# Second feed-forward of an encoder step: block products from its first pair on, and the order of the sums in front of it

## The chip, the cores and the metric

The kernel runs on one core of a Trainium2 chip. The time is device microseconds of one execution. The kernel before took 1299.93 us (median of three executions, 1299.71 to 1300.36). The profile shown below is of one further execution, which took 1300.08 us; all durations that the prediction uses come from that one.

A core has five engines that run side by side and wait for each other through semaphores: TensorE (PE in the profile) multiplies, VectorE (DVE) and ScalarE (ACT) work element by element, GpSimd (POOL) and SyncE (SP) issue transfers here. Each engine does its own instructions strictly in the order in which the program lists them.

## The reference

One layer works on 576 columns (512 frames of a new stream, 64 of a running one) of 1024 features, in float32:

```
x = x + 0.5 * swiglu(rms_norm(x, ffn1_norm))          # first feed-forward
p = rms_norm(x, mix_norm) @ w_in                       # mixer: two gated convolutions
...
merged = sigmoid(gate_a) * y_a + sigmoid(gate_b) * y_b
x = x + merged @ w_out                                 # output projection of the mixer
x = x + 0.5 * swiglu(rms_norm(x, ffn2_norm))           # second feed-forward
y = rms_norm(x, final_norm)

rms_norm(x, g) = x * rsqrt(mean(x*x) + 1e-6) * g
swiglu(h)      = (silu(h @ w_gate) * (h @ w_up)) @ w_down      # 2816 hidden features
```

The change touches the last rows of the mixer (the projection by `w_out`) and the start of the second feed-forward.

## The kernel before

**Tiling.** Features lie on the 128 partitions, so x is eight tiles `X[0..7]` of 128x576, and the 2816 hidden features are 22 tiles, in groups of 5, 5, 6 and 6. A float32 value v is split into a high part `hi` (rounded to the matmul's type) and a low part `v - hi`, and a product is three matmuls: hi·hi, hi·lo, lo·hi, where the first factor is the weight. A plain product of a weight column with all eight inputs is 8 x 3 matmuls for each half of 288 columns: 48. Its result takes one PSUM tile of two banks; there are four such tiles.

**Pairs.** For one hidden tile the gate and the up product form a 2x2 block problem: two weight columns, two halves of the input features (tiles 0 to 3 and 4 to 7), two halves of the columns. `pair` computes it with seven block products instead of eight, each of 4 x 3 = 12 matmuls into one bank: 84 in place of 96. For this DVE adds weights (sums `s1` to `s4` of the four raw weight blocks a11, a12, a21, a22), and adds inputs (the "forms" `t1` to `t4`); PE multiplies in the order a11, s2, s1, s3, a12, s4, a22 with the right sides first half of tiles 0 to 3, t2, t1, t3, first half of tiles 4 to 7, second half of tiles 4 to 7, t4; then `steps` adds the seven results on DVE and ACT (`q1`, `u2`, `u4`, `u3`, and `gate`, which multiplies by 1/rms `R` and runs Silu on ACT). The rest of a pair (`up`, `hidden`, `parts`) is left in the list `rest`, one step of which follows each block of the next pair.

**Forms.** `Forms.scale` (ACT) multiplies an input tile by its gain; `combine(p)` (four DVE instructions of 128x288, then two casts on ACT) forms the two tiles that hold t1, t2 and t3, t4 for the inputs p and p+4; `split(p)` (two DVE subtractions) makes their low parts.

**Weights.** `Stream` prepares weights in units: SP loads raw tiles of 128x512 into six buffers (`RAWS`), ACT casts the high part, and the low part is made in one of two ways. With "dma", ACT writes -hi and POOL issues a transfer that adds the raw weight to it in SBUF; with "dve", DVE subtracts. Raw tiles use the first, sums of tiles the second. `Stream.lead(n)` is called each time PE takes unit n, and issues the work of six units ahead (`AHEAD_UNITS`): this is what puts weight instructions between the others on ACT and DVE, in the order in which the program calls them.

**Around the change.** The loop over `IN_TURN` = 0, 4, 1, 5, 2, 6, 3, 7 (line 1125) is the projection by `w_out`: for each j, 48 matmuls, then DVE adds the result to `X[j]`, ACT makes the high and DVE the low part of the scaled input `xg[j]`, ACT squares `X[j]` and DVE adds the squares up; behind every second j stand scalings, forms and splits. Then `ss.gather` adds the last square and splits the sum for PE, and the second feed-forward begins with a plain product for hidden tile 0 (gate in the order of `IN_TURN`, the sum over partitions and `rstd`, up), then pairs from tile 1 on (`PLAIN["f2"]` is 1).

The calls of the engines go through a wrapper, so the profile names line 83 (85 in the changed kernel) for nearly everything; tiles tell the instructions apart: `mm` is PSUM, `x` the residual, `act` inputs and their parts, `u` and `g` (and `act`) prepared weights, `raw` loaded weights, `w` sums of weights and scaled inputs, `tmp` and `acc` intermediate values, `r` 1/rms.

Of the kernel before, what the change touches and what calls it, by code (L numbers as in the profile page):

```python
# [13 lines left out]
P = 128  # L14
D = 1024
KT = D // P
# [4 lines left out]
KU = KT // 2  # L21
T = SEQ + DSEQ
H = T // 2
# [25 lines left out]
WARM = 10  # L49


PLAIN = {"f1": 4, "f2": 1}

IN_TURN = (0, 4, 1, 5, 2, 6, 3, 7)

# [51 lines left out]
def tile_encoder_step(  # L107
# [83 lines left out]
    def par(j, r, n=1):  # L191
        return gains[:, r : r + n, j] if r < R_CA else prm[:, r - R_CA : r - R_CA + n, j]
# [129 lines left out]
    def gu_col(part, i):  # L322
        return i * P + (DFF if part == "u" else 0)

    def plan_pair(f, gu, i):

        a21, a22, a11, a12 = (
            ws.raw(gu, h * KU * P, KU, gu_col(part, i)) for part in "ug" for h in range(2)  # L330
        )
        s1, s2, s3, s4 = (f"{f}{i}s{n}" for n in range(1, 5))
        plan[f, "s", i] = [
            ws.unit(src, KU, home("g"), low, sums)
            for src, low, sums in (
                (a11, "dma", ((s1, (a21, a22)),)),
                (s2, "dve", ((s2, (s1, a11)),)),
                (s1, "dve", ()),
                (s3, "dve", ((s3, (a11, a21)),)),
                (a12, "dma", ()),  # L340
                (s4, "dve", ((s4, (s2, a12)),)),
                (a22, "dma", ()),
            )
        ]

    def plan_ffn(f, gu, dn):
# [23 lines left out]
    def plan_mixer(name, w, col):  # L370
        plan_tile(name, w, 0, (KU, KU), col, "act")
# [32 lines left out]
    def chunks(name):  # L404

        got = []
        for n in plan[name]:
            w = ws.get(n)
            got += [(w, kk) for kk in range(ws.units[n][1])]
        return got  # L410


    work = []
# [14 lines left out]
    early = {}  # L428
# [129 lines left out]
    class Forms:  # L558
# [171 lines left out]
    def ffn(f, xg, sums, finish, forms, R=None, todo=()):  # L730
# [3 lines left out]


        def plain(i, hs):
            nonlocal R
            t, up = ttile(), (f, "u", i)
            ps = product((f, "g", i), xg, order=IN_TURN if f == "f2" and i == 0 else None)
            got = None if up in early else chunks(up)  # L740
            if R is None:
                R = rstd(sums)
            ups = product(up, xg, got=got)
            hs.append(None)
            at = len(hs) - 1

            def gate():
                dve.tensor_tensor(halves(t), ps, halves(R), op=ALU.mult)
                sca.activation(t, t, AF.Silu)

            def hidden():
                dve.tensor_tensor(halves(t), ups, halves(t), op=ALU.mult)
                hs[at] = high(t)

            def parts():
                hs[at] = hs[at], low(t, hs[at])

            if f == "f2":
                rest.extend((gate, hidden, parts))
                return  # L760
            gate()
            forming()
            hidden()
            forming()
            parts()
            forming()
# [4 lines left out]
                    step(p)  # L771

        def pair(i, hs, last):
            qu, uu, t, cu = (ttile() for _ in range(4))
            q1, u2, u3, u4 = half(qu, 0), half(qu, 1), half(uu, 0), half(uu, 1)
            q = []
# [10 lines left out]
            steps = (  # L787
                lambda: sca.copy(q1, q[0]),
                lambda: dve.tensor_tensor(u2, q[1], q1, op=ALU.subtract),
                lambda: dve.tensor_tensor(u4, q[2], u2, op=ALU.subtract),  # L790
                q7,
                lambda: dve.tensor_tensor(half(t, 0), q[4], q1, op=ALU.add),
                gate,
            )
            for n, xs in enumerate(bs):
                w = ws.get(plan[f, "s", i][n])
                q.append(bank()[:, :H])
                for k in range(KU):
                    (whi, wlo), (xh, xl) = w, xs[k]
                    for m, (l, r) in enumerate(((whi, xh), (whi, xl), (wlo, xh))):  # L800
                        pe.matmul(
                            q[n], l[:, k, :], r, start=k == m == 0, stop=k == KU - 1 and m == 2
                        )
                if n > 0:
                    steps[n - 1]()
# [450 lines left out]
```

## Time and profile before

| | |
|---|---|
| median of three executions | 1299.93 us |
| profiled execution | 1300.08 us, span 1298.3 us |
| PE busy | 1286.2 us (99%), 9754 matmuls |
| DVE busy | 892.1 us (69%) |
| ACT busy | 768.7 us (59%) |
| POOL busy | 380.7 us (29%) |

The chain that ended last is 94% PE. The shares are means over the whole program; the change lies between 857 us (the projection by `w_out` begins) and about 960 us (the first group of the second feed-forward is multiplied out). The rows of the timeline that the prediction quotes give start, duration, engine, line, operation, output and inputs with their shapes, the number of instructions merged into the row, and in brackets how long the engine was idle before it and for what.

### The profile page before, as it was taken

How to read it: one execution, taken by the hardware profiler on the slowest of the kernel's cores; microseconds unless marked ns; L12 is line 12 of the kernel's file. 1: busy time of each engine (PE TensorE's matmuls, PEld its weight loads, DVE VectorE, ACT ScalarE, POOL GpSimd, SP SyncE). 2: the span in 40 equal slices, each digit the busy share in tenths (PEclk: the TensorE clock that was granted, in tenths of full speed). 3: DMA queues.
4: the chain of work that ended last, by engine and by line, in shares of the span. 5: the costliest groups of instructions: out<-in, count | busy, mean ns of one | idle time of the engine just before them, and what ended most of it. 6: DMA issues, size and time to landing. Idle time of an engine off the chain costs nothing.

```text
span 1298.3 us, 25689 instructions
## 1 busy us (share of the span) xinstructions
PE 1286.2 (99%) x9754; PEld 1283.6 (99%) x9754; DVE 892.1 (69%) x1469; ACT 768.7 (59%) x1362; POOL 380.7 (29%) x481
## 2 busy tenths in 40 slices
PE   9999999999999999999999999999999999999997
PEld 9999999999999999999999999999999999999996
DVE  6848758748945999888885160336967848847955
ACT  7746646645677654555444674467665655654664
POOL 0042332232233454333321322222142242241231
PEclk9999999999999999999999999999999999999999
DMA  7397786896698898778875978776688697796784
GB/s 219 79 196 159 157 185 155 164 196 143 151 199 180 168 212 175 169 166 177 168 168 128 197 158 174 164 157 142 139 174 175 144 194 160 155 211 133 161 176 108
DMA packets 287516, 215.39 MB, mean 166 GB/s; under 512 B 15520, under 2 KB 250016, under 8 KB 287392
## 3 DMA queue, kind: packets, MB, share of 16 engines
q0 software_dynamic: 59184, 97.28, 45.7%
q1 hardware_dynamic: 226336, 115.49, 31.4%
q8 instruction: 77, 1.26, 0.4%
q10 hardware_dynamic: 1872, 0.97, 0.3%
q14 instruction: 47, 0.39, 0.1%
HBM read 113.81 MB, written 2.62 MB: 90 GB/s over the span
## 4 chain that ended last, share of the span: by engine, by line
PE 94%; issue 2%; DVE 2%; DMA 1%; ACT 1%; POOL 0%; DVEq 0%; POOLq 0%; ACTq 0%
PE mm L83 94%; DVE tmp L83 1%; DMA u<-raw 0%; DVE g L83 0%; ACT tmp L83 0%; DMA act<-raw 0%; DMA raw<-in_ffn_w_gate_up_dram 0%; DVE x L83 0%; ACT act L83 0%; DVE acc L83 0%; ACT r L83 0%; DVE act L83 0%; ACT w L83 0%; ACT L83 0%; DVEq L1246 0%
## 5 line engine op out<-in xcount | busy, mean ns | idle before, releaser
L83 PE MATMUL mm<-act,u 128*128 128x288 f32 x4686 | 661.1, 294 | 1.2 <-DMA u<-raw 1.2
L83 PEld LDWEIGHTS mm<-act,u 128*128 128x128 f32 x4686 | 631.1, 188 | 1.7 <-DMA u<-raw 1.7
L83 PE MATMUL mm<-act,g 128*128 128x288 f32 x2778 | 399.7, 294 | 0.5 <-DMA g<-raw 0.4
L83 PEld LDWEIGHTS mm<-act,g 128*128 128x128 f32 x2778 | 378.1, 188 | 0.9 <-DMA g<-raw 0.6
L83 PE MATMUL mm<-act,act 128*128 128x288 f32 (+2 forms) x2244 | 306.7, 293 | 0.2 <-DMA act<-raw 0.2
L83 PEld LDWEIGHTS mm<-act,act 128*128 128x128 f32 x2244 | 297.6, 188 | 0.4 <-DMA act<-raw 0.4
L83 POOL DMA_DIRECT2D u<-raw x199 | 173.9, 874 | 373.0 <-ACT u L83 306.3
L83 ACT CAST u<-raw 128x512 fp32r<-128x512 f32 (+2 forms) x203 | 116.2, 572 | 165.2 <-PE mm L83 122.3
L83 POOL DMA_DIRECT2D g<-raw x122 | 106.7, 875 | 310.2 <-ACT g L83 241.4
L83 DVE SCALAR_TENSOR_TENSOR w<-g,prm,w 128x606 f32<-128x606 f32 x232 | 179.3, 843 | 1.4 <-ACT w L83 1.4
L83 DVE TENSOR_TENSOR tmp<-mm,tmp 128x288 f32<-128x288 f32 (+1 forms) x239 | 107.7, 459 | 70.2 <-PE mm L83 52.1
L83 POOL DMA_DIRECT2D act<-raw x90 | 78.0, 866 | 199.1 <-ACT act L83 195.4
L83 ACT ACTIVATE u<-u 128x512 fp32r<-128x512 f32 (+2 forms) x199 | 117.9, 593 | 6.3
L83 ACT CAST g<-raw 128x512 fp32r<-128x512 f32 (+2 forms) x126 | 68.9, 547 | 39.2 <-DMA raw<-in_ffn_w_down_dram 14.5
L83 ACT CAST u<-w 128x512 fp32r<-128x512 f32 x79 | 48.9, 619 | 60.1 <-DVE w L83 51.4
L83 DVE SCALAR_TENSOR_TENSOR tmp<-mm,r 128x576 f32<-128x576 f32 x48 | 36.3, 756 | 68.2 <-PE mm L83 68.2
L83 ACT CAST g<-w 128x512 fp32r<-128x512 f32 x77 | 47.7, 619 | 57.6 <-DVE w L83 50.1
L83 ACT CAST act<-tmp 128x576 fp32r<-128x576 f32 x84 | 56.7, 675 | 40.8 <-DVE tmp L83 39.0
L83 DVE TENSOR_TENSOR act<-tmp,act 128x576 fp32r<-128x576 f32 x84 | 62.1, 754 | 18.8 <-ACT act L83 17.2
L83 ACT ACTIVATE g<-g 128x512 fp32r<-128x512 f32 (+2 forms) x122 | 69.2, 567 | 3.9
L83 DVE TENSOR_TENSOR w<-raw,raw 128x512 f32<-128x512 f32 x78 | 53.5, 686 | 15.9 <-DMA raw<-in_ffn_w_gate_up_dram 15.9
L83 ACT CAST act<-raw 128x512 fp32r<-128x512 f32 (+3 forms) x94 | 55.6, 592 | 10.3 <-PE mm L83 7.5
(88 smaller groups left out, 804.8 us busy)
## 6 DMA issues: line engine op xcount, KB each, us to landing
raw<-in_ffn_w_gate_up_dram SPq DMA_DIRECT2D x171, 256.0 KB, 3.4
u<-raw POOLq DMA_DIRECT2D x140, 256.0 KB, 4.1
raw<-in_w_in_dram SPq DMA_DIRECT2D x112, 256.0 KB, 3.6
act<-raw POOLq DMA_DIRECT2D x80, 256.0 KB, 4.2
raw<-in_ffn_w_down_dram SPq DMA_DIRECT2D x96, 192.0 KB, 3.6
g<-raw POOLq DMA_DIRECT2D x63, 256.0 KB, 3.9
u<-raw POOLq DMA_DIRECT2D x43, 192.0 KB, 4.4
g<-raw POOLq DMA_DIRECT2D x43, 192.0 KB, 4.5
```

Of the source, the lines that this page charges most:

```text
L83: return self.tc.keep_in_program_order(fn(*args, **kwargs))
```

## The change

- `PLAIN["f2"]` goes from 1 to 0: hidden tile 0 of the second feed-forward is a pair too.
- For that one pair the blocks are taken in the order `FORMS_LAST` = 0, 4, 5, 1, 2, 3, 6, that is a11, a12, s4 (which multiply the inputs themselves), then s2, s1, s3, a22 (which multiply forms). Its weights are prepared in that order. The sum of squares goes through PE behind the sixth block, and the pair's `gate`, which needs it, moves to the head of `rest`, behind the first block of the next pair.
- In the projection loop the scaled input for the forms is made right behind each `xg[j]`, ahead of the square; `split` follows `combine` sooner; behind the loop the last `combine` and `split` come ahead of the adding of the last square (`gather`).
- The weights of `w_out` are prepared in `u` and `g` tiles in place of `u` and `act` tiles.

The core of the diff:

```diff
-PLAIN = {"f1": 4, "f2": 1}
+PLAIN = {"f1": 4, "f2": 0}
+FORMS_LAST = (0, 4, 5, 1, 2, 3, 6)
...
+    def order_of(f, i):
+        return FORMS_LAST if (f, i) == ("f2", 0) else range(7)
...
+        sums = [(s1, (a21, a22)), (s2, (s1, a11)), (s3, (a11, a21)), (s4, (s2, a12))]
+        if order == FORMS_LAST:
+            before = {0: sums[:1], 4: sums[1:2], 5: sums[3:], 3: sums[2:3]}
...
-        plan_mixer(("o", j), w_out, j * P)
+        plan_tile(("o", j), w_out, 0, (KU, KU), j * P, "g")
...
-        def scale(self, p):
-            self.b[p] = [wtile(n=T) for _ in range(2)]
-            for b, j in zip(self.b[p], (p, p + KU)):
+        def scale(self, p, js=None):
+            for j in js or (p, p + KU):
+                b = wtile(n=T)
                 sca.activation(b, X[j], AF.Copy, scale=par(j, self.r_g))
+                self.b.setdefault(p, []).append(b)
...
+            order = order_of(f, i)
+            late = ()
+            if order == FORMS_LAST:
+                steps[5], late = (lambda: None), (gate,)
+            q = [None] * 7
+            for m, n in enumerate(order):
+                q[n] = block(ws.get(plan[f, "s", i][m]), bs[n])
+                if R is None and m == 5:
+                    R = rstd(sums)
+                if m > 0:
+                    steps[order[m - 1]]()
                 if rest:
                     rest.pop(0)()
...
-            rest.extend((up, hidden, parts))
+            rest.extend((*late, up, hidden, parts))
...
+        p = n // 2
+        forms.scale(p, (j,))
         ss.square(X[j])
-        ss.add(dve)
-        p = n // 2
-        if n % 2:
-            forms.scale(p)
-        elif p > 0:
+        if n < KT - 1:
+            ss.add(dve)
+        if n % 2 == 0 and p > 0:
             forms.combine(p - 1)
-            if p > 1:
-                forms.split(p - 2)
+        if n in (3, 5, 6):
+            forms.split((n - 2) // 2)
+
+    forms.combine(KU - 1)
+    forms.split(KU - 1)
+    ss.add(dve)
     ss.gather()
-    forms.combine(KU - 1)
-    forms.split(KU - 2)
-    forms.split(KU - 1)
```

**First place: DVE, while PE makes the last product of the projection (j = 7).** Before, from the adding of the squares of `X[3]` to the low part of `xg[7]`; the `tmp` rows of 128x288 are `combine(2)`, the two `act` rows behind them a `split`, `w` a sum of weights:

```order
L83 TENSOR_TENSOR acc_1708_10688<-acc_1708_10688,tmp_1795_11221 128x576
L83 TENSOR_TENSOR tmp_1796_11224<-w_1783_11147 128x288
L83 TENSOR_TENSOR tmp_1796_11224<-w_1784_11148,tmp_1796_11224 128x288
L83 TENSOR_TENSOR tmp_1797_11225<-w_1783_11147,w_1784_11148 128x288
L83 TENSOR_TENSOR tmp_1797_11225<-w_1784_11148,tmp_1796_11224 128x288
L83 TENSOR_TENSOR act_1800_11234<-tmp_1767_11062,act_1769_11068 128x576
L83 TENSOR_TENSOR act_1801_11236<-tmp_1768_11063,act_1770_11070 128x576
L83 TENSOR_TENSOR w_1803_11239<-w_1789_11183,raw_1776_11082 128x512
L83 TENSOR_TENSOR x7_95<-mm_1802_11238,x7_95 128x576
L83 SCALAR_TENSOR_TENSOR act_1809_11299<-x7_95,gains_84,act_1808_11298 128x576
```

Now, over the same stretch (`u_1792` is the low part of s2, `w_1804` the sum s3, `g_1807` the low part of s1):

```order
L85 TENSOR_TENSOR acc_1708_10688<-acc_1708_10688,tmp_1796_11220 128x576
L85 TENSOR_TENSOR tmp_1797_11223<-w_1769_11065 128x288
L85 TENSOR_TENSOR tmp_1797_11223<-w_1784_11148,tmp_1797_11223 128x288
L85 TENSOR_TENSOR tmp_1798_11224<-w_1769_11065,w_1784_11148 128x288
L85 TENSOR_TENSOR tmp_1798_11224<-w_1784_11148,tmp_1797_11223 128x288
L85 TENSOR_TENSOR act_1801_11233<-tmp_1797_11223,act_1799_11229 128x576
L85 TENSOR_TENSOR act_1802_11235<-tmp_1798_11224,act_1800_11231 128x576
L85 TENSOR_TENSOR u_1792_11187<-w_1776_11081,u_1791_11186 128x512
L85 TENSOR_TENSOR w_1804_11239<-raw_1749_10924,raw_1734_10841 128x512
L85 TENSOR_TENSOR g_1807_11244<-w_1763_11027,g_1806_11243 128x512
L85 TENSOR_TENSOR x7_95<-mm_1803_11237,x7_95 128x576
L85 SCALAR_TENSOR_TENSOR act_1811_11300<-x7_95,gains_84,act_1810_11299 128x576
```

Between the squares and `x7` two weight subtractions have been added, and the two low parts now belong to the same `combine` (they read `tmp_1797` and `tmp_1798`, and wait for ACT's casts of those).

**Second place: ACT, behind the scaled input 7.** Before, from the high part of `xg[7]` on (`tmp_1813` is the high part of the sum of squares, `g_1804` the cast of a raw weight):

```order
L83 CAST g_1804_11241<-raw_1776_11082 128x512
L83 ACTIVATE g_1805_11242<-g_1804_11241 128x512
L83 CAST u_1806_11270<-w_1803_11239 128x512
L83 ACTIVATE act_1808_11298<-x7_95,gains_84 128x576
L83 ACTIVATE tmp_1810_11302<-x7_95 128x576
L83 ACTIVATE w_1811_11304<-x3_91,gains_84 128x576
L83 ACTIVATE w_1812_11305<-x7_95,gains_84 128x576
L83 CAST tmp_1813_11308<-acc_1708_10688 128x576
```

Now (`g_1827`, `g_1828` are the high part and -hi of a22 of the first pair):

```order
L85 ACTIVATE act_1810_11299<-x7_95,gains_84 128x576
L85 ACTIVATE w_1812_11303<-x7_95,gains_84 128x576
L85 ACTIVATE tmp_1813_11305<-x7_95 128x576
L85 CAST act_1816_11313<-tmp_1814_11307 128x576
L85 CAST act_1817_11315<-tmp_1815_11308 128x576
L85 CAST tmp_1820_11321<-acc_1708_10688 128x576
L85 CAST g_1827_11333<-raw_1737_10872 128x512
L85 ACTIVATE g_1828_11334<-g_1827_11333 128x512
```

The casts of the last forms and of the sum of squares now stand ahead of the weight a22.

**Third place: ACT, at the first Silu of the second feed-forward.** Now (`tmp_1824` is the gate of the first pair, `raw_1840` is a11 of the third pair):

```order
L85 ACTIVATE r_1851_11454<-tmp_1849_11452 128x576
L85 CAST g_1853_11466<-w_1846_11433 128x512
L85 CAST u_1861_11491<-raw_1766_11034 128x512
L85 ACTIVATE u_1862_11492<-u_1861_11491 128x512
L85 ACT_TABLE_LOAD
L85 ACTIVATE tmp_1824_11328<-tmp_1824_11328 128x576
L85 CAST g_1867_11519<-raw_1840_11397 128x512
L85 ACTIVATE g_1868_11520<-g_1867_11519 128x512
```

Before, the row behind the table load was the Silu of the plain tile, and a cast of a raw weight stood behind that in the same way:

```order
L83 ACTIVATE r_1838_11406<-tmp_1836_11404 128x576
L83 CAST g_1846_11473<-raw_1763_11028 128x512
L83 ACTIVATE g_1847_11474<-g_1846_11473 128x512
L83 ACT_TABLE_LOAD
L83 ACTIVATE tmp_1823_11331<-tmp_1823_11331 128x576
L83 CAST u_1853_11501<-raw_1826_11336 128x512
L83 ACTIVATE u_1854_11502<-u_1853_11501 128x512
```

What moved here is the Silu's place in the work: its inputs are now complete only behind the last block of the first pair, and the program lists it behind the first block of the second.

More of the change, by code (lines that the diff above doesn't have):

```diff
@@ L325, in plan_pair, with plan_block @@
     def plan_pair(f, gu, i):
-        a21, a22, a11, a12 = (
+        plan_block((f, "s", i), [
             ws.raw(gu, h * KU * P, KU, gu_col(part, i)) for part in "ug" for h in range(2)
-        )
[L332 to L343, printed above, removed]
+        ], [home("g") for _ in range(7)], order=order_of(f, i))
+    def order_of(f, i):
+        return FORMS_LAST if (f, i) == ("f2", 0) else range(7)
+    def plan_block(name, raws, homes, order=range(7)):
+        a21, a22, a11, a12 = raws
+        s1, s2, s3, s4 = ((name, n) for n in range(1, 5))
+        units = (
+            (a11, "dma"), (s2, "dve"), (s1, "dve"), (s3, "dve"), (a12, "dma"), (s4, "dve"),
+            (a22, "dma"),
+        )
+        sums = [(s1, (a21, a22)), (s2, (s1, a11)), (s3, (a11, a21)), (s4, (s2, a12))]
+        if order == FORMS_LAST:
+            before = {0: sums[:1], 4: sums[1:2], 5: sums[3:], 3: sums[2:3]}
+        else:
+            before = {0: sums[:1], 1: sums[1:2], 3: sums[2:3], 5: sums[3:]}
+        plan[name] = [
+            ws.unit(units[n][0], KU, home, units[n][1], before.get(n, ()))
+            for n, home in zip(order, homes)
         ]
@@ L410, in chunks, with block @@
         return got
+    def block(w, xs):
+        q = bank()[:, :H]
+        for k in range(KU):
+            (whi, wlo), (xh, xl) = w, xs[k]
+            for m, (l, r) in enumerate(((whi, xh), (whi, xl), (wlo, xh))):
+                pe.matmul(q, l[:, k, :], r, start=k == m == 0, stop=k == KU - 1 and m == 2)
+        return q
     work = []
@@ L736, in plain @@
         def plain(i, hs):
-            nonlocal R
             t, up = ttile(), (f, "u", i)
[L739 to L743, printed above, removed]
+            ps = product((f, "g", i), xg)
+            ups = product(up, xg)
             hs.append(None)
@@ L756, in parts @@
                 hs[at] = hs[at], low(t, hs[at])
-            if f == "f2":
-                rest.extend((gate, hidden, parts))
-                return
             gate()
@@ L785, in gate @@
                 sca.activation(t, t, AF.Silu)
-            steps = (
+            steps = [
                 lambda: sca.copy(q1, q[0]),
@@ L793, in pair @@
                 gate,
[L794 to L805, printed above, removed]
+            ]
+            order = order_of(f, i)
[9 more added lines that the diff above has]
+                    steps[order[m - 1]]()
                 if rest:
```

2 lines of the change are left out of this document (1 added, 1 removed).

## The prediction

> **What bounds the kernel now.** First the page: what is busy, and the chain of waits.
>
> ```profile
> PE 1286.2 (99%) x9754; PEld 1283.6 (99%) x9754; DVE 892.1 (69%) x1469; ACT 768.7 (59%) x1362; POOL 380.7 (29%) x481
> PE 94%; issue 2%; DVE 2%; DMA 1%; ACT 1%; POOL 0%; DVEq 0%; POOLq 0%; ACTq 0%
> ```
>
> PE sets the end, so every matmul taken away is a gain, and every moment in which PE waits is a loss. Second, PE's own waits, and two stretches of 20 us, of which the first holds these waits (columns: PE, PEld, DVE, ACT and POOL busy with counts, granted clock, DMA share, GB/s).
>
> ```profile
> PE mm L83 <- DMA u<-raw: 1.2, 2, 0.8
> PE mm L83 <- DMA g<-raw: 0.4, 1, 0.4
> 60.00:80.00 20.00, 18.41 (x134) 17.71 (x133) 9.78 (x18) 13.54 (x31) 9.51 (x12) 1.00 0.84 166
> 920.00:940.00 20.00, 20.00 (x152) 19.92 (x151) 18.39 (x34) 13.62 (x25) 4.30 (x5) 1.00 0.72 163
> ```
>
> These 1.6 us, 18.41 busy of 20, lie where the first feed-forward goes over to pairs. At the same place in the second feed-forward PE does not wait at all; its timeline:
>
> ```profile
> 900.72 0.94 PE L83 MATMUL mm<-act,g 128*128 128x288 f32 x6
> ...
> 906.97 0.69 PE L83 MATMUL mm<-tmp,ones_r 128*128 128x288 f32 x4
> 907.50 3.32 PE L83 MATMUL mm<-act,g 128*128 128x288 f32 x24
> ...
> 913.82 1.74 PE L83 MATMUL mm<-act,g 128*128 128x288 f32 x12
> 915.39 1.76 PE L83 MATMUL mm<-act,u 128*128 128x288 f32 x12
> 917.00 1.74 PE L83 MATMUL mm<-act,g 128*128 128x288 f32 x12
> ```
>
> At 900.72 the projection has ended; the plain gate takes 6.25 us, the plain up product 6.32 us, and a block of 12 takes 1.57 or 1.61 us, 1.59 in the mean. Third, what feeds PE here, DVE:
>
> ```profile
> 894.68 0.76 DVE L83 TENSOR_TENSOR x<-mm,x 128x576 f32<-128x576 f32 x1 [1.92 <-PE mm L83]
> 896.29 0.82 DVE L83 SCALAR_TENSOR_TENSOR act<-x,gains,act 128x576 fp32r<-128x576 f32 x1 [0.85 <-ACT act L83]
> 897.02 0.75 DVE L83 TENSOR_TENSOR acc<-acc,tmp 128x576 f32<-128x576 f32 x1
> 897.69 0.45 DVE L83 TENSOR_TENSOR tmp<-w 128x288 f32<-128x288 f32 x1
> ...
> 899.29 1.42 DVE L83 TENSOR_TENSOR act<-tmp,act 128x576 fp32r<-128x576 f32 x2
> 900.63 0.68 DVE L83 TENSOR_TENSOR w<-w,raw 128x512 f32<-128x512 f32 x1
> 901.23 0.75 DVE L83 TENSOR_TENSOR x<-mm,x 128x576 f32<-128x576 f32 x1
> 902.83 0.82 DVE L83 SCALAR_TENSOR_TENSOR act<-x,gains,act 128x576 fp32r<-128x576 f32 x1 [0.85 <-ACT act L83]
> 903.57 0.75 DVE L83 TENSOR_TENSOR acc<-acc,tmp 128x576 f32<-128x576 f32 x1
> 905.31 0.76 DVE L83 TENSOR_TENSOR tmp<-acc,tmp 128x576 fp32r<-128x576 f32 x1 [0.99 <-ACT tmp L83]
> ```
>
> With its last rows before the projection's end DVE has no slack left: from 896.29 it is idle only where it waits for ACT, and `X[7]` is added at 901.23, half a us behind PE. The low part of `xg[7]` ends at 903.65. That was early enough, because the plain gate needs input 7 only in its last 6 of 48 matmuls, at 906.2: 2.5 us to spare. This margin is what the change spends.
>
> **The saving.** 96 matmuls in 6.25 + 6.32 = 12.57 us become 7 blocks of 1.59 us = 11.13 us. Saved: 1.44 us. The four matmuls of the sum stay.
>
> **A: input 7 (PE at the second block).** Block a11 takes inputs 0 to 3, block a12 inputs 4 to 7; the second matmul of input 7 needs its low part and is the 23rd, at 900.72 + 22 x 0.132 = 903.6. When is it there? ACT's part of such an input, now:
>
> ```profile
> 902.02 0.78 ACT L83 ACTIVATE act<-x,gains 128x576 fp32r<-128x576 f32 x1
> 902.70 0.68 ACT L83 ACTIVATE tmp<-x 128x576 f32<-128x576 f32 x1
> 903.28 1.44 ACT L83 ACTIVATE w<-x,gains 128x576 f32<-128x576 f32 x2
> ```
>
> The high part starts 0.8 behind the adding of x (901.23), the square 0.68 later, then the scalings, about 0.67 each.
> - While j = 6 is worked off, DVE has 1.92 us idle ahead of 894.68. Two subtractions of 128x576 come in (0.67 each by 897.02 to 897.69: 1.35); the squares now stand behind one more scaling on ACT (0.67 more, of which about 0.5 is not covered), here and one j earlier: 1.0. So the adding of `X[3]` slips by 1.35 + 1.0 - 1.92 = 0.4, to 895.1.
> - Low part 1.6 later (894.68 to 896.29): 896.7. The square ends at 895.1 + 0.8 + 3 x 0.68 = 897.9, so its adding starts there, then 0.67, then the four form instructions 1.6 (897.69 to 899.29): 900.2. Their high parts come from ACT at 900.3 and 901.0, so the two low parts end at 901.7. Then three instructions of 128x512 in place of one, 0.60 each (900.63 to 901.23): `X[7]` is added at 903.5.
> - 1.6 us later (901.23 to 902.83) the low part starts: 905.1. It ends at 905.95.
>
> PE waits 905.95 - 903.6 = **2.3 us**. Without the slip at j = 6 and with the square hidden it would be 1.5, the low end.
>
> **B: the weight s3.** Its subtraction is listed behind the sum of squares. From 905.1: 0.73 and the forms 1.6, at 907.4; low parts, with ACT's second cast, to 908.9; adding the last square, then the low part of the sum 1.74 later (903.57 to 905.31) and 0.68: 911.3; s3 ends 0.69 later, 912.0. PE wants it at 905.95 + 0.25 + 3 blocks + 0.25 = 911.2. Wait: **0.8 us** (0 to 1.2).
>
> **C: the weight a22.** ACT and POOL:
>
> ```profile
> 914.88 0.60 ACT L83 CAST g<-raw 128x512 fp32r<-128x512 f32 x1
> 915.52 0.63 ACT L83 ACTIVATE g<-g 128x512 fp32r<-128x512 f32 x1
> 916.17 1.28 ACT L83 ACT_TABLE_LOAD   x1
> 919.26 0.69 ACT L83 ACTIVATE tmp<-tmp 128x576 f32<-128x576 f32 x1 [1.81 <-DVE tmp L83]
> 919.85 0.60 ACT L83 CAST u<-raw 128x512 fp32r<-128x512 f32 x1
> 916.44 0.86 POOL L83 DMA_DIRECT2D g<-raw  x1 [1.84 <-ACT g L83]
> DMA to landing us min/median/max: 3.3/3.9/6.0
> ```
>
> From the cast of a raw weight to POOL's issue are 1.56 us (914.88 to 916.44), and 3.9 more to its landing (the last row, of the `u` tiles between 905 and 960 us). The cast of a22 stands behind the cast of the sum of squares, which starts 0.8 behind 908.9: cast at 910.4, issue 912.0, landing 915.9. PE, released at 912.05, needs 10 matmuls, the sum (0.53) and two more: 914.15. Wait: **1.7 us** (1.1 at a landing of 3.3, 3.8 at 6.0). The Trainium skill, "DMA: Bandwidth & Descriptors", section "Anatomy of one DMA", fits such a transfer as 2.0 us plus its bytes at 436 GB/s, as an estimate 2.6 us for 256 KB; by that this wait would be 0.4. The trace's 3.3 to 6.0 disagrees and decides.
>
> **D: a free bank.** The chain from the sum to R:
>
> ```profile
> 913.50 0.75 DVE L83 TENSOR_SCALAR tmp<-mm 128x576 f32<-128x576 f32 x1
> 917.27 0.69 DVE L83 TENSOR_TENSOR u<-w,u 128x512 fp32r<-128x512 f32 x1
> ```
>
> It takes 3.77 us. DVE reaches it behind seven weight instructions, two additions and short waits for ACT (about 5.3 us from 911.9), and ends it at 921.0; `u3` and the next addition, which free the bank of s1 and s3, stand behind it and end at 922.3. PE, released at 915.9, has 10 matmuls and three blocks: 921.9, and then needs that PSUM tile. Wait: **0.5 us** (0 to 1.2).
>
> **E: a weight behind the Silu.** From 922.3 DVE does two weight instructions, an addition and the product with R (2.4 us): Silu starts at 924.75. Behind it on ACT is the cast of a11 of the third pair (919.26 to 919.85: 0.6), then 1.56 and 3.9: landing at 930.8. PE has four blocks and two matmuls from 922.4: 929.0. Wait: **1.85 us** (1.2 to 4). **F:** a22 of the third pair stands behind the next Silu in the same way; DVE is busy 18.39 of 20 us from 920 to 940, so it wins back at most about 1 us in a pair of 11.1: **0.9 us** (0 to 1.8). Later pairs wait for nothing.
>
> The `w_out` weights in other tiles cost nothing: units are prepared six ahead, 18.7 us at 3.12 us each, which hides them; without it a wait for one landing, 3.9.
>
> Sum: 2.3 + 0.8 + 1.7 + 0.5 + 1.85 + 0.9 = 8.05, less 1.44: **+6.6 us**, on 1300.08 us (0.15 above the median, which lies 1.6 above the span): 1306.7 us.
>
> **Rivals.**
> 1. Only A is paid: PE, 2.3 us late, gives the later chains their time back. 2.3 - 1.44 = +0.9: 1301.0 us. Against it, B to F are counted from a PE already late, and DVE and ACT are late by the same. Chance 0.09.
> 2. Other side: nothing is waited for, -1.44: 1298.6 us. For it speaks that PE waits for nothing here today, and that the 1.6 us of the first feed-forward are all its waits for `u` and `g` transfers. It needs `X[7]` added by 901.2, as today, with 3.5 us more work ahead of it; the time falls below before's once all waits sum to under 1.44. Chance 0.05.
> 3. Another rhythm. PE's spacing changes at such sums:
>
> ```profile
> 716.07 3.33 PE L83 MATMUL mm<-act,u 128*128 128x288 f32 x24
> 719.23 0.69 PE L83 MATMUL mm<-tmp,ones_r 128*128 128x288 f32 x4
> 719.76 3.28 PE L83 MATMUL mm<-act,act 128*128 128x288 f32 x24
> 722.88 3.28 PE L83 MATMUL mm<-act,u 128*128 128x288 f32 x24
> ```
>
> 3.16 us for 24 ahead, 3.12 behind; at 906.97 it goes the other way. The sum now stands elsewhere; were the second feed-forward to run at 3.12 (1.56 a block), 356 us would lose 5.6: 1301.1 us. No block anywhere in the trace runs so. Chance 0.05.
> 4. Slow landings: at 6.0 us C and E cost 2.1 more each: 1310.9 us. It was one landing of many. Chance 0.04.
> 5. A slower clock behind the waits: half speed for 3.4 us would add 1.7: 1308.4 us. The Trainium skill, "TensorE: Matmul & The Clock Gate", section "What's actually happening", has the clock halved after an idle window of about 3.4 us. The row from 60 to 80 us shows 1.00 granted across 1.6 us of waits; the longest here is 2.3. Chance 0.02.
>
> **How the numbers follow.** The forecast, waits at several of A to F that sum to 4 to 10 us, has 0.75. From the bounds alone: A 1.5, C 1.1, E 1.2 and the others nothing is +2.4; with all upper ends 2.3 + 1.2 + 3.8 + 1.2 + 4 + 1.8 - 1.44 is +12.9, but a longer landing at C shortens D. The range 1300.8 to 1309.8 takes in rivals 1, 3 and 5 and leaves out 2, 4 and some of the forecast's edges; the forecast's own range is 1302.5 to 1309.8. A change under 0.2% (2.6 us) can hardly be told from none in a measurement of this kernel. Slower: 0.80 (the forecast nearly whole, 4 and 5). Same: 0.18 (1, 2, 3 and the forecast's low edge). Faster: 0.02, rivals 2 and 3 together.
>
> **What would show it.** Right: 9742 matmuls; PE idle inside the second block of the second feed-forward for about 2.3 us, ended by DVE or ACT on `act`; `X[7]` added some 2.8 us behind PE; then a wait for a `g` transfer of 1 to 2 us at the seventh block, one for DVE in the second pair, one or two for transfers behind Silu; spacing of blocks as before. Wrong: `X[7]` added within a us, or PE's waits from 900 to 940 us summing to under 4 us.

## The result, and the profile after

The changed kernel took 1306.58 us (median of five executions, 1306.17 to 1308.14); the kernel before, beside it, 1299.93 us (1299.62 to 1301.67). The medians differ by 6.65 us; the ratio of the two kernels is 1.0054, with a 95% interval from 1.0043 to 1.0065, so the changed kernel is slower. The profiled execution took 1306.52 us, with a span of 1304.7 us (before: 1298.3).

Every "Measured" below gives a median of five executions (where it is another number, it is said) and the ratio to the kernel before, measured beside it, with its 95% interval. Two single executions, 1391.58 us of light2 and 2572.4 us of after_again, lie far off all others of their kernels: the ratios leave them out, the medians count them (without them 1301.76 and 1307.21 us).

The page of the changed kernel: the engines' busy time, and the chain that ended last.

```profile
PE 1287.1 (99%) x9742; PEld 1282.8 (98%) x9742; DVE 899.7 (69%) x1484; ACT 769.6 (59%) x1365; POOL 381.0 (29%) x480
PE 69%; issue 16%; DMA 6%; DVE 4%; POOL 2%; ACT 2%; POOLq 0%; SPq 0%; DVEq 0%; ACTq 0%
```

Twelve matmuls are gone (9754 before), and yet PE is busy 0.9 us longer. Its share of the chain falls from 94% to 69%: other engines now stand in it. PE's timeline from 899 to 941 us, where it waited for nothing before:

```profile
899.92 1.74 PE L85 MATMUL mm<-act,g 128*128 128x288 f32 x12
901.49 1.34 PE L85 MATMUL mm<-act,u 128*128 128x288 f32 x9
904.61 0.40 PE L85 MATMUL mm<-act,u 128*128 128x288 f32 x1 [1.77 <-ACT act L85]
905.46 0.54 PE L85 MATMUL mm<-act,u 128*128 128x288 f32 x2 [0.46 <-DVE act L85]
905.84 2.67 PE L85 MATMUL mm<-act,g 128*128 128x288 f32 x12
908.31 2.40 PE L85 MATMUL mm<-act,u 128*128 128x288 f32 x12
910.55 1.74 PE L85 MATMUL mm<-act,g 128*128 128x288 f32 x12
...
914.24 0.42 PE L85 MATMUL mm<-act,g 128*128 128x288 f32 x2
914.93 1.60 PE L85 MATMUL mm<-act,g 128*128 128x288 f32 x10 [0.27 <-DMA g<-raw]
...
922.06 1.82 PE L85 MATMUL mm<-act,g 128*128 128x288 f32 x12 [0.77 <-DVE tmp L85]
...
928.49 0.43 PE L85 MATMUL mm<-act,g 128*128 128x288 f32 x2
930.24 1.58 PE L85 MATMUL mm<-act,g 128*128 128x288 f32 x10 [1.32 <-DMA g<-raw]
...
940.21 1.61 PE L85 MATMUL mm<-act,g 128*128 128x288 f32 x10 [0.19 <-DMA g<-raw]
```

The projection ends at 899.92. The wait inside the second block is there (1.77 for the high part of input 7, 0.46 for its low part), then one at the last block, one for DVE at 922.06, and two for transfers, behind the first Silu and the next. One thing isn't a wait: the two blocks from 905.84 to 910.55 take 4.71 us in place of 3.18, and PE is not idle in them. The window from 905 to 910 us shows why (behind the busy times and counts of the five engines stands the granted clock):

```profile
905.00:910.00 5.00, 4.54 (x23) 4.54 (x23) 4.13 (x8) 2.77 (x6) 0.00 (x0) 0.66 0.12 35
```

The clock fell to 0.66 behind the wait; in the 5 us before it was 1.00. In windows of 1 us it is 0.50 from 907 to 909 us, where products start 0.24 us apart in place of 0.132.

### The profile page after: what moved, and what is told of

The parts are those of the page before. It is cut to its first block, busy times and chain, and to the rows that moved or that the text cites. A ratio compares the mean times of both kernels' runs of the same rounds, so it can differ in the third digit from the quotient of the medians.

```text
span 1304.7 us, 25691 instructions
## 1 busy us (share of the span) xinstructions
PE 1287.1 (99%) x9742; PEld 1282.8 (98%) x9742; DVE 899.7 (69%) x1484; ACT 769.6 (59%) x1365; POOL 381.0 (29%) x480
## 4 chain that ended last, share of the span: by engine, by line
PE 69%; issue 16%; DMA 6%; DVE 4%; POOL 2%; ACT 2%; POOLq 0%; SPq 0%; DVEq 0%; ACTq 0%
PE mm L85 69%; DMA g<-raw 2%; POOL u L85 1%; DVE tmp L85 1%; DMA raw<-in_ffn_w_down_dram 1%; DMA u<-raw 1%; POOL g L85 1%; DMA raw<-in_ffn_w_gate_up_dram 1%; DVE act L85 1%; DVE acc L85 1%; ACT act L85 1%; ACT tmp L85 1%; DVE g L85 1%; DMA x<-in_x_dram 0%; DVE x L85 0%
## 5 line engine op out<-in xcount | busy, mean ns | idle before, releaser
L85 PE MATMUL mm<-act,g 128*128 128x288 f32 x2958 | 426.5, 295 | 4.9 <-DMA g<-raw 4.1
L85 PEld LDWEIGHTS mm<-act,g 128*128 128x128 f32 x2958 | 402.6, 188 | 7.0 <-DMA g<-raw 5.7
L85 POOL DMA_DIRECT2D u<-raw x201 | 178.4, 889 | 366.0 <-ACT u L85 304.0
L85 PE MATMUL mm<-act,act 128*128 128x288 f32 (+2 forms) x2052 | 279.8, 293 | 0.0
L85 PEld LDWEIGHTS mm<-act,act 128*128 128x128 f32 x2052 | 271.8, 188 | 0.0
L85 POOL DMA_DIRECT2D g<-raw x127 | 114.1, 900 | 357.2 <-ACT g L85 287.9
L85 POOL DMA_DIRECT2D act<-raw x82 | 71.3, 870 | 164.9 <-ACT act L85 164.4
L85 ACT CAST g<-raw 128x512 fp32r<-128x512 f32 (+2 forms) x131 | 71.9, 549 | 40.0 <-DMA raw<-in_ffn_w_gate_up_dram 21.3
L85 ACT ACTIVATE g<-g 128x512 fp32r<-128x512 f32 (+2 forms) x127 | 72.3, 569 | 4.0
L85 ACT ACTIVATE tmp<-tmp 128x576 f32<-128x576 f32 x47 | 32.2, 685 | 45.9 <-DVE tmp L85 45.8
```

The lines of the kernel that those rows point to most:

```text
L85: return self.tc.keep_in_program_order(fn(*args, **kwargs))
```

## The experiments

Two theories stood against each other. **Theory 1, the chain:** DVE and ACT go through a fixed list from the projection's last products to the first Silu, and never wait for PE on the way; so they, and not PE's waits, set when the second pair and the weights behind the Silu come. Taking one wait off PE changes nothing, and taking work off that list does. **Theory 2, the sum:** each wait, and the low clock, costs by itself. What speaks for theory 1 in the trace is DVE's own waits from 894 to 923.4 us in the changed kernel

```profile
DVE act L85 <- ACT act L85: 1.7, 2, 0.9
DVE tmp L85 <- ACT tmp L85: 0.8, 1, 0.8
DVE tmp L85 <- ACT r L85: 0.8, 1, 0.8
DVE acc L85 <- ACT tmp L85: 0.4, 1, 0.4
DVE g L85 <- ACT g L85: 0.3, 1, 0.3
```

beside this row for the same stretch before, which is gone now:

```profile
DVE x L83 <- PE mm L83: 1.9, 1, 1.9
```

DVE now waits for ACT alone.

### One wait filled, and the old loop

**fill16** puts 16 products where PE waits for input 7. Their results go to a bank that the next block overwrites.

```
         q = bank()[:, :H]
         for k in range(KU):
+            if fill and k == KU - 1:
+                spare.insert(0, bank())
+                for _ in range(fill):
+                    pe.matmul(spare[0][:, :H], w[0][:, 0, :], xs[0][0], start=True, stop=True)
...
+                fill = 16 if order == FORMS_LAST and m == 1 else 0
```

> The changed kernel with 16 more products of 288 columns (16 x 0.132 = 2.1 us), whose results are overwritten, put where TensorE waits for the last input's high and low part in the second block. TensorE is busy through that wait, so the granted clock should stay at 1.00 in the 5 us behind it, where it was 0.66. Theory 1: the 1.55 us that the low clock cost come back as waits for the two low weights and the cast behind them (0.8 and 1.6 us at their places), and the time stays 1306.2 to 1307.0. Theory 2, each loss counts by itself: 1.55 us less, 1305.0.

Measured: 1307.62 us, 1.0061 (1.0048 to 1.0074) of the kernel before. PE's timeline, and the window from 905 to 910 us:

```profile
900.30 1.74 PE L85 MATMUL mm<-act,g 128*128 128x288 f32 x12
901.88 3.58 PE L85 MATMUL mm<-act,u 128*128 128x288 f32 x26
...
911.89 1.58 PE L85 MATMUL mm<-act,u 128*128 128x288 f32 x10 [0.47 <-DVE u L85]
...
915.30 1.59 PE L85 MATMUL mm<-act,g 128*128 128x288 f32 x10 [1.03 <-DMA g<-raw]
...
922.45 1.82 PE L85 MATMUL mm<-act,g 128*128 128x288 f32 x12 [0.80 <-DVE tmp L85]
905.00:910.00 5.00, 4.62 (x35) 4.39 (x34) 4.52 (x8) 2.76 (x5) 0.00 (x0) 1.00 0.21 64
```

The clock stays at 1.00, and the 1.5 us that it had cost come back as two waits, for a low weight on DVE and for the last block's weight. From the projection's end to the block that waits for a bank are 922.45 - 900.30 = 22.15 us; in the changed kernel it is 922.06 - 899.92 = 22.14. Theory 2's 1305.0 is out. The median is 0.6 us above theory 1's range all the same. In the profiled execution, which took 1308.23 us, PE waits 1.38 us at 942.00 for one more transfer, the one for which it waited 0.19 in the changed kernel; whether the other executions have this too is not shown.

**pair_only** has the old order of scalings, squares and forms in the projection's loop, and the change's pair (the lines of the new order, which go, are not shown).

```
...
+        ss.add(dve)
+        p = n // 2
+        if n % 2:
+            forms.scale(p)
+        elif p > 0:
+            forms.combine(p - 1)
...
+    ss.gather()
     forms.combine(KU - 1)
...
```

> The changed kernel with the old loop order of the projection (the sum gathered before the last forms). Theory 1, the chain of DVE and ACT sets the end and not where its pieces stand: waits of about 1.2 us at the seventh input and 2.9 us at the last forms in place of the change's, the same end, 1306.0 to 1307.0. Theory 2, each wait counts by itself, and the new loop order saves what it takes off the forms: 1.5 us or more over the changed kernel, 1308 or later.

Measured: 1307.04 us, 1.0056 (1.0044 to 1.0069), at the upper end of theory 1's range. PE waits 0.40 and 0.46 us at input 7 and then for the last forms:

```profile
900.25 1.74 PE L85 MATMUL mm<-act,g 128*128 128x288 f32 x12
...
909.10 0.66 PE L85 MATMUL mm<-act,u 128*128 128x288 f32 x3 [1.62 <-DVE act L85]
910.44 0.85 PE L85 MATMUL mm<-act,u 128*128 128x288 f32 x2 [0.68 <-DVE act L85]
...
922.26 1.82 PE L85 MATMUL mm<-act,g 128*128 128x288 f32 x12
```

Other waits, and 22.01 us to the same block. The clock fell here too (0.66 from 910 to 915 us), and PE came to the block just as the bank was free, so this row shows no wait. That the end is the same is therefore better read on DVE: it begins the reciprocal root at 917.06, 16.81 us behind the projection's end, and 16.93 us behind it in the changed kernel (916.85 - 899.92). For the total the order in the loop does not matter here once the pair is there; it decides only which instruction PE is waiting at.

**after_again** is the changed kernel once more, for the comparisons that follow.

> The changed kernel itself, for the comparisons of this call: 1306.2 to 1307.2. If the drop of the granted clock behind the wait for the last input comes in some executions only, its profile may show 1.00 there; then the waits for the two low weights and the cast (0.5 and 1.0 us) stand in its place and the end is the same within 0.5 us.

Measured: 1307.32 us, 1.0056 (1.0043 to 1.0069), 0.1 us above the range expected. This profile has the clock at 1.00 in every window of 5 us from 900 to 925 us, after the same waits at input 7:

```profile
900.55 1.74 PE L85 MATMUL mm<-act,g 128*128 128x288 f32 x12
...
905.25 0.40 PE L85 MATMUL mm<-act,u 128*128 128x288 f32 x1 [1.77 <-ACT act L85]
906.10 0.53 PE L85 MATMUL mm<-act,u 128*128 128x288 f32 x2 [0.46 <-DVE act L85]
...
912.15 1.59 PE L85 MATMUL mm<-act,u 128*128 128x288 f32 x10 [0.48 <-DVE u L85]
...
915.56 1.60 PE L85 MATMUL mm<-act,g 128*128 128x288 f32 x10 [1.02 <-DMA g<-raw]
...
922.70 1.82 PE L85 MATMUL mm<-act,g 128*128 128x288 f32 x12 [0.79 <-DVE tmp L85]
```

22.15 us again. The same program shows the drop in one execution and not in another, and in each of the two measurements executions with a mean clock of 0.996 stand beside others with 0.998. So the drop is a matter of chance, and the end does not feel it here: with the drop the two weights arrive while PE is still at work, without it PE waits for them.

### The loop alone, and a clock that does count

**loop_only** is the kernel before with the new loop order; the first tile keeps its 96 products. The weights of `w_out` stand in the change's tiles here as well. The lines are shown against the changed kernel:

```
-PLAIN = {"f1": 4, "f2": 0}
+PLAIN = {"f1": 4, "f2": 1}
...
+            if R is None:
+                R = rstd(sums)
+            ups = product(up, xg, got=got)
```

> The kernel before with the projection's new loop order alone (products, sums and low parts in the order of the change), its first tile of 96 products kept. Theory 1, the chain: the loop's new order puts the last low part and the last square later, so the first products on the sum of squares wait 2 to 3 us, and the time is 1.5 to 3 us over the kernel before: 1301.4 to 1303. Theory 2, the price lies in the pair of blocks alone: within 0.5 us of the kernel before, 1299.4 to 1300.4.

Measured: 1305.17 us, from 1302.52 to 1305.88; 1.0042 (1.0028 to 1.0056). Both theories missed: the median is 2 us above theory 1's upper end, and only the profiled execution, 1302.52 us, lies in its range. There PE waits 2.21 + 0.39 us for the sum of squares, at a clock of 1.00, and for nothing else up to 962 us. Since the longer executions also had a lower mean clock (0.995 and 0.996 against 0.997), two kernels were to tell whether the clock drops behind this wait too.

> The kernel with the new loop order alone once more, for its profile. Theory 1: if its time is over 1304, the 5 us behind the wait for the sum of squares show a granted clock near 0.66 and blocks of 12 products of 2.2 to 2.8 us in place of 1.6; if it is under 1303, they show 1.00. Theory 2: a long execution with the clock at 1.00 there.

The same kernel again, one execution: 1305.36 us. The same waits, then the clock, as theory 1 had it:

```profile
909.32 0.40 PE L83 MATMUL mm<-tmp,ones_r 128*128 128x288 f32 x1 [2.20 <-ACT tmp L83]
...
910.62 4.88 PE L83 MATMUL mm<-act,g 128*128 128x288 f32 x24
915.33 3.33 PE L83 MATMUL mm<-act,u 128*128 128x288 f32 x24
910.00:915.00 5.00, 4.88 (x25) 4.88 (x26) 4.12 (x8) 3.07 (x5) 0.86 (x1) 0.66 0.40 111
```

24 products take 915.33 - 910.62 = 4.71 us in place of 3.17. That is 1.54 of the 2.84 us between the two executions; 0.26 lies ahead of it (the projection ends later), and most of the rest is a wait of 0.8 us for a transfer at the kernel's end.

**loop_fill** keeps PE busy with 18 products ahead of the sum.

```
+            for _ in range(fill):
+                pe.matmul(p[:, 0, :H], terms[0][0], xg[0][0][:, :H], start=True, stop=True)
...
-                R = rstd(sums)
+                R = rstd(sums, fill=18 if f == "f2" else 0)
```

> The kernel with the new loop order alone, and 18 more products of 288 columns, whose results are overwritten, at the place where TensorE waits for the sum of squares (2.21 + 0.39 us there). Theory 1: the executions of the loop order alone spread from 1302.5 to 1305.9 because the granted clock drops behind that wait in some of them, and there nothing behind it waits and takes the loss up; with TensorE busy it can't drop, so the median is 1302.0 to 1303.0 and the spread under 1.5 us. Theory 2, the spread has another source: the median stays near 1305 and the spread at 3 us.

Measured: 1302.51 us (median of eleven), 1.0022 (1.0013 to 1.0030); executions from 1301.43 to 1303.44, all with a mean clock of 0.997 or 0.998. The median is where theory 1 had it; the spread, 2.0 us, is wider than the 1.5 that it allowed, and narrower than the 3.4 without the products. With useless work in the place of a wait the median is 2.7 us lower, of which the rows above account for 1.54; the other 1.1 us are not traced. Here no later wait stands behind the low clock to swallow it.

### Links of the chain

**dma_lows** takes the subtractions for the low parts of the first pair's weight sums off DVE (four: the expectation counts three); POOL's transfers make them.

```
+        if order == FORMS_LAST:
+            units = tuple((src, "dma") for src, _ in units)
```

> The changed kernel with the low parts of the first pair's three weight sums made by POOL's DMA in place of DVE (three operations of about 0.68 us on DVE less before the first gate, and three casts less on ACT are not: the casts stay). Theory 1: DVE's queue sets the end, so about 1.5 us less than the changed kernel, 1305.0, although TensorE's waits for weights get no shorter. Theory 2, the waits for DMA count by themselves: three more landings of 3.9 us on the path, the same or later, 1306.5 to 1308.

Measured: 1304.50 us, 1.0038 (1.0025 to 1.0050), 0.5 us under theory 1. PE's waits for `g` transfers between 893 and 962 us did not get shorter (2.3 us in all, 1.8 in the changed kernel), as theory 1 said. From the projection's end to the second pair's bank are 20.63 us, 1.5 less:

```profile
899.91 1.74 PE L85 MATMUL mm<-act,g 128*128 128x288 f32 x12
...
920.54 1.82 PE L85 MATMUL mm<-act,g 128*128 128x288 f32 x12 [0.28 <-DVE tmp L85]
```

**r_short** leaves out the step that refines the reciprocal root.

```
+        if bare:
+            return r
         dve.scalar_tensor_tensor(t, y, -0.5, y, op0=ALU.mult, op1=ALU.mult)
...
-                    R = rstd(sums)
+                    R = rstd(sums, bare=True)
```

> The changed kernel with the last three DVE operations of the reciprocal root left out in the second feed-forward (the step that refines it; 918.35, 919.14 and 919.93 in the changed kernel's trace, 2.3 us); the output is that of the unrefined root. Theory 1, DVE's queue up to the first gate sets the end: the wait of 0.8 us for the banks goes, the Silu comes 2.3 us earlier and the wait of 1.3 us for the third pair's weight goes with it: 2.0 to 3.0 us less than the changed kernel in the same call. Theory 2, only the wait for the banks is the reciprocal root's, and the weight's is the landing's: 0.8 us less.

Measured: 1303.56 us, 1.0031 (1.0019 to 1.0043), 3.8 us under after_again, more than theory 1's 2.0 to 3.0. Between the two profiled executions (1303.08 and 1307.10 us) are 4.0 us, of which 1.1 lie ahead of the change (this projection ends at 899.44, that one at 900.55); the remaining 2.9 are theory 1's. Between 893 and 962 us the wait for DVE's `tmp` is gone, and of the transfers only the last block's is left:

```profile
PE mm L85 <- ACT act L85: 1.8, 1, 1.8
PE mm L85 <- DMA g<-raw: 1.0, 1, 1.0
PE mm L85 <- DVE u L85: 0.5, 1, 0.5
PE mm L85 <- DVE act L85: 0.5, 1, 0.5
```

So the wait of 1.3 us behind the Silu was not the landing's: the cast behind the Silu feeds the same transfer, and with an earlier Silu the wait isn't there.

**no_squares** leaves out the squares of six inputs.

```
-        ss.square(X[j])
-        if n < KT - 1:
-            ss.add(dve)
+        if n in (0, KT - 1):
+            ss.n = n
+            ss.square(X[j])
```

> The changed kernel with the squares of six of the eight inputs left out of the projection's loop (six operations on ACT, six additions on DVE); the sum of squares and so the output are wrong by that. Theory 1: ACT and DVE get to the last input earlier, the wait of 1.8 us for its high part goes, the chain behind it moves up by as much: 1.4 to 2.2 us less than the changed kernel in the same call. Theory 2, the chain to the gate is set by the weights' operations and not by where the input's end: 0.5 us less or nothing.

Measured: 1305.09 us, 1.0040 (1.0028 to 1.0052), 2.2 us under after_again, at theory 1's upper end. The wait for the high part is gone, and the second pair's bank comes 20.22 us behind the projection's end (900.48 and 920.70) in place of 22.15: 1.9 of the 2.2 us.

**silu_late** moves the first pair's Silu one block on.

```
+                if order_of(f, i) != FORMS_LAST:
+                    sca.activation(t, t, AF.Silu)
...
+            def silu():
                 sca.activation(t, t, AF.Silu)
...
-                steps[5], late = (lambda: None), (gate,)
+                steps[5], late = (lambda: None), (gate, silu)
```

> The changed kernel with the first pair's Silu one block later on ACT, behind the cast of the third pair's first weight. Theory 1: it takes one link of 0.7 us with its wait of 3 us for the gate's product out of the chain to the weight of the third pair, the wait of 1.3 us there goes, and nothing behind takes it up: 1.2 to 1.8 us less than the changed kernel, 1304.8 to 1305.4. Theory 2, the DMA's landing is what is late there: the same time, 1306.2 to 1307.

Measured: 1306.08 us (1304.99 to 1306.40), 1.0047 (1.0034 to 1.0059). By the time this is unsettled: it lies between the two theories, and its interval overlaps the changed kernel's. The trace is plain: the wait of 1.3 us for the third pair's weight is gone, and nothing behind it up to 962 us has come in its place; the profiled execution took 1304.99 us. The changed kernel was not measured beside it, so the size of the gain is left open between 0.5 and 1.6 us.

### A shorter chain altogether

**lighter_chain** has four edits: `"dma"` low parts for the sums of the first three pairs, the squares' additions on POOL, the sum gathered inside the first pair, and a later Silu in the first two pairs.

```
+        if name[0] == "f2" and name[2] < 3:
+            units = tuple((src, "dma") for src, _ in units)
...
+            later = f == "f2" and i < 2
...
+                if R is None and m == 1:
+                    sums.gather()
...
-            ss.add(dve)
+            ss.add(pool)
```

> The changed kernel with a shorter chain on DVE and ACT: the low parts of the first three pairs' weight sums by POOL's DMA, the squares' additions on POOL, the sum gathered inside the first pair (behind its second block), and the Silu of the first two pairs one block later. Theory 1: the waits come down to 0.7 and 1.1 us and the 1.4 us of the 12 products fewer pay for them: within 1 us of the kernel before, 1299 to 1300.5. Theory 2, the waits are those of the landings and of the clock and only move: 1303 or later.

Measured: 1305.11 us, 1.0040 (1.0027 to 1.0054). Theory 1 missed by 4.6 us; the time lies where theory 2 had it, in a kernel with four edits at once. There is no wait for a bank any more, but beside the waits at input 7 (0.9 + 0.5 us) PE now waits for the low parts that were given to POOL's transfers (893 to 962 us):

```profile
PE mm L85 <- DMA u<-w: 1.7, 2, 1.1
PE mm L85 <- DMA g<-w: 1.7, 1, 1.7
```

**light2** leaves them to POOL in the first pair only (`name[2] < 1`).

> The shorter chain again, with POOL's DMA making the low parts of the first pair's three weight sums alone, those of the second and third pair back on DVE. Theory 1: the 3.4 us that the shorter chain waited for those low parts were landings in a full queue; they go, and waits of about 1 and 1.2 us for DVE come at the banks: 1 to 2 us over the kernel before, 1300.5 to 1302. Theory 2, the landings aren't the queue's load: waits for DMA of over 1 us stay, and the time is over 1303.5.

Measured: 1301.90 us (median of twelve), 1.0016 (1.0007 to 1.0025), as theory 1 had it. The two kernels' landings of `u` tiles issued by POOL from 905 to 940 us, first lighter_chain, then light2, and the DMA engines' share from 915 to 920 us (next to last column):

```profile
DMA to landing us min/median/max: 3.8/6.6/7.9
915.00:920.00 5.00, 2.97 (x21) 2.51 (x19) 3.18 (x6) 4.87 (x9) 3.26 (x4) 1.00 1.13 235
```

```profile
DMA to landing us min/median/max: 3.5/4.3/4.8
915.00:920.00 5.00, 4.18 (x30) 3.74 (x28) 4.18 (x7) 3.96 (x8) 1.72 (x2) 1.00 0.69 160
```

The first row of lighter_chain counts raw weights and sums, that of light2 raw weights alone. For transfers of raw weights only, the medians are 6.4 us (`u`) and 7.0 (`g`) in lighter_chain, 4.3 and 3.7 in light2. The two kernels differ only in the eight low parts, so it is these that the queue had no room for. PE's waits in light2 up to 962 us are 0.8 + 0.5 at input 7 and 0.6 + 0.9 for banks, 2.8 in all. Against after_again, measured beside it, it wins back 5.4 of 7.7 us, and it is still slower than the kernel before. No version here is faster than that.

## Why the prediction was right, point by point

The time was forecast at 1306.7 and came out at 1306.58. The waits came where they were forecast (B and C in full only in after_again). That the total is this close is luck in part, since the terms miss by 0.25 to 1.2 us each, on both sides. What each step was worth is read from starts on PE's timeline: a product starts 0.132 us behind the one before, and whatever lies beyond that is lost. At A: nine products from 901.49 put the next start at 902.68, and it came at 904.61, 1.93 late; the one behind it 0.72 late. Behind each wait one more spacing is 0.1 too long, which is added in. All in us:

| step | predicted | changed kernel's profile (clock 0.66) | after_again (clock 1.00) |
|---|---|---|---|
| A, input 7 | 2.3 | 2.75 | 2.75 |
| B, weight s3 | 0.8 | 0 | 0.75 |
| C, weight a22 | 1.7 | 0.55 | 1.3 |
| low clock (rival 5) | 1.7, at 0.02 | 1.55 | 0 |
| D, a free bank | 0.5 | 1.0 | 1.0 |
| E, weight behind the Silu | 1.85 | 1.6 | 1.6 |
| F, the next one | 0.9 | 0.45 | 0.4 |
| sum | 8.05 | 7.9 | 7.8 |

Less the saving of 1.44 us (9742 matmuls, blocks of 1.57 to 1.6 us as before) the changed kernel's profile gives +6.45; the spans differ by 6.4. The waits alone, as PE's rows from 900 to 940 us show them, sum to 4.6 us in that profile and to 5.8 in after_again, both above the 4 us below which the prediction was to count as wrong; the rest of the table is the low clock and what a wait costs beyond its row.

- **A** held in kind: the wait stands in the second block. Two of DVE's rows, the addition of `X[7]` and the first operation of the reciprocal root:

```profile
903.00 0.75 DVE L85 TENSOR_TENSOR x<-mm,x 128x576 f32<-128x576 f32 x1
916.85 0.75 DVE L85 TENSOR_SCALAR tmp<-mm 128x576 f32<-128x576 f32 x1
```

  `X[7]` is added 3.08 us behind the projection's end; 2.8 was forecast. The 0.3 come from the turn before: `X[3]` is added 5.34 us ahead of the projection's end (894.58), where it had been 6.04, a slip of 0.7 in place of 0.4. That PE waits already for the high part, and then again for the low one, was not said.
- **B and C** hold in after_again, C at 1.3 in place of 1.7. In the profile first taken they had shrunk, since PE itself was slow: the wait of 1 to 2 us at the seventh block, named as a sign of being right, is 0.27 there and 1.02 in after_again.
- **D** was put at half its size, **F** at twice. (D's own times, 922.3 against 915.9 + 1.32 + 3 x 1.59 = 921.99, give 0.3 and not 0.5.) E's cause, the weight's cast behind the Silu, is shown by r_short and silu_late, which take the wait away without touching the transfer.
- That the later chains don't give PE its time back, which the prediction held against **rival 1**, was the step that decided, and it was only half argued there: "DVE and ACT are late by the same". The runs show it in numbers. From the addition of `X[7]` to the first operation of the reciprocal root DVE takes 916.85 - 903.00 = 13.85 us in the changed kernel, and as much in fill16, where PE worked through the wait:

```profile
903.38 0.75 DVE L85 TENSOR_TENSOR x<-mm,x 128x576 f32<-128x576 f32 x1
917.24 0.75 DVE L85 TENSOR_SCALAR tmp<-mm 128x576 f32<-128x576 f32 x1
```

  So the terms A to D don't add up because each is a price: they add up because together they are DVE's lateness, whichever of them PE meets. E and F lie behind, at weights that ACT casts only after a Silu; there the traces show the wait come and go, and what E is worth in time stays between 0.5 and 1.6 us (silu_late).
- **Rival 5**, given 0.02, happened in the profile of the changed kernel, and did not give its 1308.4: the loss came out of B and C. To price it as an addition was wrong for this kernel, and right for loop_only, at 1.54 us in place of 1.7.
- **Rival 2** is out by every run. **Rival 3:** PE's rhythm did not change (by its own rows, 3.16 and 3.12 us, it would have been worth 4.5 us and not 5.6). **Rival 4** did not come here; lighter_chain shows landings as long, with eight more transfers in the queue.
- "Later pairs wait for nothing" was wrong. Over the whole program PE waits 4.1 us for `g` transfers; 1.8 of that lie in the stretch above, 1.4 in the first feed-forward (the kernel before waits 1.6 there), and about 0.9 behind 1000 us. These 0.9 did not show in the sum, since this execution happened to reach the projection's end 0.8 us before that of the kernel before.

```profile
PE mm L85 <- DMA g<-raw: 4.1, 7, 1.3
```

The new loop order by itself, with no product fewer, costs 5.7 us in the median (loop_only), and still 3.0 where idle products hold the clock up (loop_fill): the sum of squares comes too late for the plain tile.

## What to carry to other kernels

Where PE waits several times in a row, ask first whether the engine that feeds it ever waits for PE in between. If it doesn't, PE's waits are one lateness seen at several places, and removing one, or filling it, moves it to the next. Here only work taken off the feeding engine's list, or put behind the point where PE needs it, moved the end. Where nothing waited behind a gap of 2 us, it cost 1.5 more through the clock in some executions, and idle products in it were worth their place.

## What the runs showed of the hardware

- **The clock fell after waits of 2.2 to 2.6 us in two pieces.** In seven profiles with waits of 1.6 to 2.2 us and another of 0.4 to 0.7 close behind, the granted clock was 0.66 in the next 5 us three times (the changed kernel, pair_only, loop_again) and 1.00 four times (after_again, silu_late, r_short, loop_only), with the same program and the same waits in two cases. In windows of 1 us it falls to 0.50, and 0.66 over 5 us is 0.34 x 5 / 0.5 = 3.4 us at half speed. That costs 1.55 us and not 1.7, since products then start 0.24 us apart, 1.8 times 0.132 and not twice. In light2 and lighter_chain, with 0.85 + 0.46, it stayed at 1.00. The Trainium skill, "TensorE: Matmul & The Clock Gate", section "What's actually happening", has the clock halved after an idle window of about 3.4 us that runs freely. The length at half speed agrees, and so does the chance. That a whole idle window is needed does not: PE was never idle for more than 2.2 us at a stretch ahead of these drops.
- **A wait costs more than its row.** The row of 1.77 us delays the next start by 1.93, 0.46 by 0.72, 0.27 by 0.43, 1.32 by 1.49: 0.16 to 0.26 us each, before the 0.1 of the next spacing. Most of it is how the rows are counted: a product stands as busy for 0.29 us in them, and the next one, had it not waited, would have started 0.132 us after it, which leaves 0.16.
- **POOL's transfers landed late in a full queue:** those of raw weights for `u` tiles took 6.4 us in place of 4.3 once the low parts of three pairs and not of one (256 KB each) were among them. From 915 to 940 us the DMA share was 1.07 to 1.13 then, and 0.41 to 0.96 in light2.
